# Experts' activations multiplied by their gates in halves of 128 tokens, the first half during the gates' stage; flags summed on VectorE; a deeper list pipeline

## The chip, the cores and the metric

The kernel runs on one core of a Trainium2 chip. What counts is the device time of one execution in microseconds; of several executions of one kernel the median is taken. Below, TensorE is PE in the profile, VectorE is DVE, ScalarE is ACT, GpSimd is POOL, and SP issues the weight loads.

## The reference, cut to what matters

256 tokens with 2048 features pass one attention block, then a layer of 16384 tiny experts, then a second block (a gated recurrence and projections). The change touches the middle layer alone:

```python
q = (xt @ w_query).reshape(T, 8, 2, 128)
scores = jnp.einsum('thpc,hpnc->thpn', q, sub_keys)
vals, idx = lax.top_k(scores, 16)
cand = (vals[..., 0, :, None] + vals[..., 1, None, :]).reshape(T, 8, 256)
top_vals, top_c = lax.top_k(cand, 16)
experts = (i1 * 128 + i2).reshape(T, 128)
gates = jax.nn.softmax(top_vals, axis=-1).reshape(T, 128)
hdn = gelu(einsum('ted,td->te', expert_down[experts], xc))
y = einsum('te,ted->td', gates * hdn, expert_up[experts])
```

## The kernel before, in words

The kernel does not gather the rows of `expert_down`. It multiplies the normalised tokens by all 16384 rows, takes the gelu, and multiplies by a gate matrix that is zero where a token did not choose an expert. Rows of `expert_up` are gathered, but only of experts that some token chose.

**Stream.** Every weight comes as a unit of 1 MB (`Stream`, L48). SP loads it into one of three `raw` tiles; ACT casts each half to a high part (L74) and DVE subtracts that part to get the low one (L75); five half tiles `whl` are in turn. `next()` makes the halves a unit needs, `used()` makes one more half after the unit's matmuls. `fm` (L91) then issues 48 matmuls of 256 columns (L100 to L102) for a unit.

**Order of the work.** Small steps beside the matmuls stand in a list `k.bg`. After each unit `pump` runs one step, and `pump_by(k, us)` (L172) runs steps against a credit: the unit gives `us`, each step takes the price it is declared with. `after(k, n, f)` puts f off by n pumps, `drain` runs all that is left. Every engine works its own instructions in the order in which they were written; nothing reorders them.

**The stages of the middle layer** (`phase_peer`, L563):
1. 16 query units. Scores go to the two-step top-16 on DVE (`topk`, L605). During the 16th unit the activations `act` are rewritten in place in four quarters (`split`, L209, from a copy `xr` scaled on POOL), each once the unit's matmuls of that quarter are done; the expert units read the new ones.
2. 128 expert units (`ORDER`, four units to a group j of 512 experts; JS=31 is the last group but one to be computed). Each unit's result passes the gelu on ACT (L982, in `hidden`).
3. Beside them, the gates' stage: 64 steps `place_steps` (L726), four tokens each: one-hot tiles on DVE (L690, L691), gates put in on ACT and DVE (L698, L700), four matmuls, copy on ACT (L717), addition on DVE (L722). After four steps the 16 tokens' tile `gst` (two in turn) goes to `used` (L736): POOL issues a store to `g_d` in HBM, and a DMA that adds the tile onto `fsum`; after eight tiles DVE reduces `fsum` to flags F (L744).
4. Beside the later expert units, the lists: 32 steps `lists_steps` (L848), each with one-hot tiles on DVE (L826, L828), ACT (L836) and DVE (L837) putting keys in, and four matmuls of 200 columns (L845). In step q the one-hots are those of q+2, the keys those of q+1, the matmuls those of q. What is left at unit 123 is drained.
5. A group of activations that is finished before all gates are placed is stored to `gh_d`; it is "late". Afterwards `catch_up` (L998) loads late groups and their gates again (`load_late`, `load_g`), multiplies them on POOL (`times`, L880) and stores them to `hm_d` (L883). Groups finished later are multiplied at once in `hidden`. JS is kept in SBUF as `hst` and split there, at once.
6. `overflow` (L1058) is a loop for more chosen experts than the lists hold, skipped if there are none; all engines read the count and branch. DVE computes two small tiles (L1060, L1062) ahead of the branch.
7. Four units of `expert_up` for JS and 100 gathered units (L1117).

Of the kernel before, what the change touches and what calls it, by code (L numbers as in the profile page):

```python
# [9 lines left out]
F32 = mybir.dt.float32  # L10
# [16 lines left out]
NE = 128  # L27
# [20 lines left out]
class Stream:  # L48
# [514 lines left out]
def phase_peer(k, A):  # L563
# [5 lines left out]
    with ExitStack() as ctx:  # L569
# [78 lines left out]
        slot, F = {}, []  # L648
# [30 lines left out]
        fsum = pp.tile([128, 128, 16], F32, name="fsum", tag="gtd")  # L679
# [141 lines left out]
        def lists_hot(q):  # L821
            cs = slice(4 * q, 4 * q + 4)
            a = pw.tile([128, 4, 128], F32R, name="oa", tag="oa", bufs=3)
# [8 lines left out]
        def lists_keys(q):  # L832
            cs = slice(4 * q, 4 * q + 4)
            b = pw.tile([128, 4, 2, KT], F32R, name="ob", tag="ob")
            e = hot[q][1]
            nc.scalar.mul(b[:, :, 0, :], e, pi)  # L836
            nc.vector.tensor_mul(b[:, :, 1, :], e, iota[:, cs, None].to_broadcast([128, 4, KT]))  # L837
            hot[q][1] = b

        def lists_fill(q):  # L840
# [3 lines left out]
            for j in range(4):  # L844
                nc.tensor.matmul(L["ps"][:, :2 * KT], a[:, j, :], b[:, j].rearrange("p e r -> p (e r)"),  # L845
                                 start=q + j == 0, stop=q == 31 and j == 3)

        def lists_steps(q):  # L848
# [4 lines left out]
            lists_fill(q)  # L853
# [17 lines left out]
        Gs, late = {}, deque()  # L871

        def load_g(m, tag):
            gt = pp.tile([128, 16, 128], F32, name="gt", tag=tag)
            nc.gpsimd.dma_start(gt, g_d[:, :, m * 128:(m + 1) * 128].rearrange("g p x -> p g x"))
# [6 lines left out]
        def store(j, gh):  # L882
            nc.gpsimd.dma_start(hm_d[1 + 512 * j:1 + 512 * (j + 1), :].rearrange("(a p) t -> p a t", p=128), gh)  # L883

        def load_late(j):
            if j // 2 not in Gs:
                Gs.clear()
                Gs[j // 2] = load_g(j // 2, "gst%d" % (j // 2 % 2))
            x = pp.tile([128, 4, 256], F32, name="ght", tag="ght%d" % (j % 3))
            nc.gpsimd.dma_start(x.rearrange("p a t -> p (a t)"), gh_d[j])  # L890
            return x, Gs[j // 2]
# [5 lines left out]
        scaled = []  # L897
        for g in range(16):
            w = st.next()
            acc = bank(k, "acc")[:, :256]  # L900
            if g == 15:
                for q in range(4):
                    fm(k, acc, w, k.act, part=(4 * q, 4 * q + 4))
                    qs = slice(4 * q, 4 * q + 4)
                    split(k, k.act[0][:, qs, :], k.act[1][:, qs, :], scaled.pop(0))
            elif g == 0:
# [16 lines left out]
            if g < 2:  # L923
                pump(k)
            else:
                pump_by(k, 3.2)
# [11 lines left out]
        state = {}  # L938

        def prepare():  # L940
# [30 lines left out]
            yield step(1.5, lambda: lists_hot(0))  # L971
            yield step(2.2, lambda: (lists_hot(1), lists_keys(0)))
            for q in range(32):
                yield step(2.2, lambda q=q: lists_steps(q))
# [5 lines left out]

        def hidden(j, a, gh, acc):
# [3 lines left out]
            if "placed" not in state:  # L985
                nc.scalar.dma_start(gh_d[j], gh.rearrange("p a t -> p (a t)"))
                late.append(j)
                return
            if state.get("g") != j // 2:
# [722 lines left out]
```

## Time and profile before

| | us |
|---|---|
| median of 3 runs | 2737.36 (lowest 2737.03) |
| the profiled execution | 2741.86 |
| its span, first to last instruction | 2740.1 |
| PE busy | 2634.3 (96%) |
| DVE busy | 1829.5 (67%) |
| ACT busy | 1411.4 (52%) |
| POOL busy | 738.6 (27%) |

The profiled execution is 4.5 us above the median, and 1.8 us of it lie outside the span. Busy shares are means over stages that differ; a stretch of the trace tells more. Where matmuls follow each other without a gap, their count in 50 us says how fast PE really went.

### The profile page before, as it was taken

What the parts mean: (1) busy time and instruction counts of PE and PEld (TensorE: products, weight loads), DVE (VectorE), ACT (ScalarE), POOL (GpSimd) and SP (SyncE); (2) the same over time, 40 slices, a digit from 0 to 9 for tenths busy, and PEclk for the clock granted to TensorE, in tenths of its full rate; (3) what the DMA queues carried; (4) which work ended last, traced back from release to release, by engine and by line L of the source; (5) the groups of instructions that cost most, each with busy time, mean ns of one, the idle gap of its engine ahead of it and who ended that gap; (6) DMA issues with size and microseconds to landing.
All of it is one profiled execution on the core that took longest, in us unless ns stands there. A gap on an engine that the chain in (4) does not pass through costs nothing. (4 is left out here: it accounts for less than half of the span.)

```text
span 2740.1 us, 44958 instructions
## 1 busy us (share of the span) xinstructions
PE 2634.3 (96%) x18008; PEld 2409.1 (88%) x18008; DVE 1829.5 (67%) x2685; ACT 1411.4 (52%) x2302; POOL 738.6 (27%) x779
## 2 busy tenths in 40 slices
PE   8999999989999999989759999999999999999997
PEld 8977778989999999989748888887999999999886
DVE  5554455899777877688826666666568775555555
ACT  6344455544566666434325555556665544444453
POOL 0001011532000000255625555645145540000000
PEclk9999999999999999999879999999999999999999
DMA  7433435456688888989847888885544445555553
GB/s 290 169 123 139 155 118 188 155 171 214 208 279 274 279 279 289 312 308 340 303 146 271 297 292 293 293 300 173 191 167 156 153 154 204 185 185 188 185 192 127
DMA packets 95268, 599.11 MB, mean 219 GB/s; under 512 B 11536, under 2 KB 11664, under 8 KB 31952
## 3 DMA queue, kind: packets, MB, share of 16 engines
q1 hardware_dynamic: 53696, 381.05, 39.6%
q0 software_dynamic: 36608, 200.23, 21.6%
q10 hardware_dynamic: 4752, 14.92, 1.5%
q8 instruction: 143, 2.34, 0.3%
q14 instruction: 69, 0.57, 0.1%
HBM read 532.19 MB, written 47.19 MB: 211 GB/s over the span
## 5 line engine op out<-in xcount | busy, mean ns | idle before, releaser
L75 DVE TENSOR_TENSOR whl<-raw,whl 128x1024 fp32r<-128x1024 f32 (+2 forms) x917 | 1188.5, 1306 | 633.7 <-ACT whl L74 623.0
L74 ACT CAST whl<-raw 128x1024 fp32r<-128x1024 f32 (+2 forms) x917 | 954.3, 1048 | 734.2 <-PE acc L102 381.4
L100 PE MATMUL acc<-act,whl 128*128 128x256 f32 x3840 | 1083.4, 282 | 17.8 <-ACT whl L74 17.6
L101 PE MATMUL acc<-act,whl 128*128 128x256 f32 x3840 | 1081.8, 282 | 9.1 <-DVE act L214 8.7
L102 PE MATMUL acc<-act,whl 128*128 128x256 f32 x3840 | 1081.6, 282 | 0.8 <-DVE whl L75 0.8
L100 PEld LDWEIGHTS acc<-act,whl 128*128 128x128 f32 x3840 | 729.4, 190 | 20.2 <-ACT whl L74 17.8
L101 PEld LDWEIGHTS acc<-act,whl 128*128 128x128 f32 x3840 | 730.1, 190 | 10.0 <-DVE act L214 8.9
L102 PEld LDWEIGHTS acc<-act,whl 128*128 128x128 f32 x3840 | 733.3, 191 | 1.3 <-DVE whl L75 1.3
L1117 PE MATMUL acc<-whl,hh 128*128 128x512 f32 x864 | 218.2, 396 | 0.0
L1117 PE MATMUL bg<-whl,hh 128*128 128x512 f32 x864 | 217.9, 396 | 0.0
L118 PE MATMUL acc<-whl,act 128*128 128x512 f32 (+1 forms) x512 | 198.2, 387 | 6.9 <-ACT whl L74 6.9
L119 PE MATMUL acc<-whl,act 128*128 128x512 f32 (+1 forms) x512 | 196.1, 383 | 4.0 <-DVE whl L75 3.9
L1117 PEld LDWEIGHTS bg<-whl,hh 128*128 128x128 f32 x864 | 162.5, 188 | 39.3
L1117 PEld LDWEIGHTS acc<-whl,hh 128*128 128x128 f32 x864 | 162.4, 188 | 39.2
L120 PE MATMUL acc<-whl,act 128*128 128x512 f32 (+1 forms) x512 | 195.8, 382 | 0.8 <-DVE act L217 0.8
L1047 POOL DMA_INDIRECT raw<-in_up,idx_l x100 | 134.1, 1341 | 150.5 <-DVE hh L895 77.6
L118 PEld LDWEIGHTS acc<-whl,act 128*128 128x128 f32 x512 | 97.5, 190 | 28.7 <-ACT whl L74 7.4
L119 PEld LDWEIGHTS acc<-whl,act 128*128 128x128 f32 x512 | 97.5, 190 | 24.4 <-DVE whl L75 5.8
L738 POOL DMA_DIRECT2D g_d<-gst x16 | 8.9, 556 | 395.7 <-DVE gst L722 395.7
L120 PEld LDWEIGHTS acc<-whl,act 128*128 128x128 f32 x512 | 97.4, 190 | 20.2 <-DVE act L217 1.0
L1047 POOL DMA_INDIRECT hr<-hm_d,idx_l x100 | 104.4, 1044 | 31.0 <-issue 30.7
L700 ACT ACTIVATE ob<-oe,sl_g 128x128 fp32r<-128x128 f32 x256 | 81.5, 391 | 8.1 <-ACT ghs L982 6.5
(407 smaller groups left out, 3071.5 us busy)
## 6 DMA issues: line engine op xcount, KB each, us to landing
raw<-in_down SPq DMA_DIRECT2D x128, 1024.0 KB, 6.3
raw<-in_w_cv SPq DMA_DIRECT2D x32, 1024.0 KB, 4.8
raw<-in_w_gg SPq DMA_DIRECT2D x32, 1024.0 KB, 4.8
raw<-in_w_dil SPq DMA_DIRECT2D x24, 1024.0 KB, 4.9
gt<-g_d POOLq DMA_DIRECT2D x17, 1024.0 KB, 10.7
raw<-in_w_out SPq DMA_DIRECT2D x16, 1024.0 KB, 4.8
raw<-in_w_pq SPq DMA_DIRECT2D x16, 1024.0 KB, 4.9
g_d<-gst POOLq DMA_DIRECT2D x16, 1024.0 KB, 7.8
```

The lines of the kernel that those rows point to most:

```text
L74: nc.scalar.copy(hi[:, s], r[:, s])
L75: nc.vector.tensor_sub(lo[:, s], r[:, s], hi[:, s].bitcast(F32))
L100: k.nc.tensor.matmul(acc, hi[:, f], x, start=j == 0, stop=False)
L101: k.nc.tensor.matmul(acc, hi[:, f], y, start=False, stop=False)
L102: k.nc.tensor.matmul(acc, lo[:, f], x, start=False, stop=j == nk - 1)
L118: k.nc.tensor.matmul(accs[t], ah[:, kk, ts], hi[:, m], start=st, stop=False)
L119: k.nc.tensor.matmul(accs[t], ah[:, kk, ts], lo[:, m], start=False, stop=False)
L120: k.nc.tensor.matmul(accs[t], al[:, kk, ts], hi[:, m], start=False, stop=sp)
L700: nc.scalar.mul(b[:, j, 0, :], e[:, j, :], slot["g"][:, 0, 4 * q + j:4 * q + j + 1].bitcast(F32))
L738: nc.gpsimd.dma_start(g_d[g], x.rearrange("p i t -> p (i t)"))
L1047: nc.gpsimd.indirect_dma_start(out=out, out_offset=None, in_=table, in_offset=bass.IndirectOffsetOnAxis(ap=idx, axis=0), bounds_check=n - ...
L1117: nc.tensor.matmul(accs[2 * s + c][t], x[:, ts], y[:, c * 512:(c + 1) * 512], start=i == 0 and x is hh and y is hi, stop=last_ and i == N - 1)
```

## The change

- `used`: no DMA onto `fsum`. DVE reduces each 16-token tile itself (128x2048 to 128x128) and adds the result to F. After tile 7 the first 128 tokens' gates count as placed (`placed0`), after tile 15 the others (`placed1`).
- The late groups are handled by halves of 128 tokens, with two lists. A first half may be loaded, multiplied and stored from `placed0` on, in two units of three, while the gates' stage still runs; second halves from `placed1` on, as before. Gate tiles are halves too; for a group multiplied at once, the next pair's gates are loaded as soon as the current pair is used.
- The lists: both key columns are put in by ACT (six instructions a step where there was one; DVE's L837 goes); the matmuls in step q are those of q-1; buffers are added under other tiles' tags; the declared price of a step falls from 2.2 to 1.7. Two of three waiting steps ahead of the lists go.
- JS's split into `hst` comes three pumps later.
- The last two query units run as a pair, quarter by quarter, so each quarter of `act` is rewritten while both go on; the two units get one step of background each.
- `overflow`: the two tiles are computed inside the branch.

```diff
         def used(g, x):
             nc.gpsimd.dma_start(g_d[g], x.rearrange("p i t -> p (i t)"))
-            if g % 8 == 0:
-                nc.gpsimd.dma_start(fsum, x)
-            else:
-                nc.gpsimd.dma_start(fsum, x, accum_op=OP.add)
+            f = F[g // 8] if g % 8 == 0 else pw.tile([128, 128], F32, name="fg", tag="tk")
+            nc.vector.tensor_reduce(f, x, axis=AX.X, op=OP.add)
+            if g % 8:
+                nc.vector.tensor_add(F[g // 8], F[g // 8], f)
             if g % 8 == 7:
-                after(k, 3, lambda: nc.vector.tensor_reduce(F[g // 8], fsum, axis=AX.X, op=OP.add))
+                state["placed%d" % (g // 8)] = True
...
         def lists_keys(q):
-            b = pw.tile([128, 4, 2, KT], F32R, name="ob", tag="ob")
+            if q % 3 == 2:
+                b = [pw.tile([128, 2, 2, KT], F32R, name="ob", tag="oh") for _ in range(2)]
+            else:
+                b = pw.tile([128, 4, 2, KT], F32R, name="ob", tag="ob")
+                b = [b[:, 0:2], b[:, 2:4]]
             e = hot[q][1]
-            nc.scalar.mul(b[:, :, 0, :], e, pi)
-            nc.vector.tensor_mul(b[:, :, 1, :], e, iota[:, cs, None].to_broadcast([128, 4, KT]))
+            for i in range(2):
+                nc.scalar.mul(b[i][:, :, 0, :], e[:, 2 * i:2 * i + 2], pi)
+            for j in range(4):
+                nc.scalar.mul(b[j // 2][:, j % 2, 1, :], e[:, j, :], float(4 * q + j))
...
-            lists_fill(q)
+            if q >= 1:
+                lists_fill(q - 1)
...
-        def load_late(j):
...
+        def load_late(j, t):
+            if j // 2 not in Gs[t]:
+                Gs[t].clear()
+                Gs[t][j // 2] = load_g(j // 2, t, "gst%d" % (j // 2 % 2) if t else "gtd", 1 if t else 2)
+            x = pp.tile([128, 4, 128], F32, name="ght", tag="ght%d" % (lates[0] % 3))
+            lates[0] += 1
+            nc.gpsimd.dma_start(x, gh_d[j].rearrange("p (a t) -> p a t", t=256)[:, :, t * 128:(t + 1) * 128])
+            return x, Gs[t][j // 2]
...
+                pair = [(acc, w), (bank(k, "acc")[:, :256], st.peek())]
                 for q in range(4):
-                    fm(k, acc, w, k.act, part=(4 * q, 4 * q + 4))
+                    for o, x in pair:
+                        fm(k, o, x, k.act, part=(4 * q, 4 * q + 4))
+                    if q == 1:
+                        st.used()
+                        st.used()
...
-            for q in range(32):
-                yield step(2.2, lambda q=q: lists_steps(q))
+            for q in range(33):
+                yield step(1.7, lambda q=q: lists_steps(q))
...
+            n = ORDER.index(j) + 1
+            if n < 32 and ORDER[n] // 2 != j // 2:
+                state["g"], state["gt"] = ORDER[n] // 2, [load_g(ORDER[n] // 2, t, "gtd", 2) for t in range(2)]
             if j == JS:
...
-                split(k, hst[:, 0], hst[:, 1], gh)
+                after(k, 3, lambda: split(k, hst[:, 0], hst[:, 1], gh))
...
+            n = 0
+            if "placed1" in state:
+                n = -(-(len(late[0]) + len(late[1])) // max(1, NE - 6 - i))
+            elif "placed0" in state and i % 3 < 2:
+                n = 1
...
-            nc.vector.tensor_scalar(d, d, -128.0 * KT, None, op0=OP.add)
...
-            with k.tc.If(turns > 0), k.tc.For_i(0, turns, 1) as _:
+            with k.tc.If(turns > 0):
+                nc.vector.tensor_scalar(d, d, -128.0 * KT, None, op0=OP.add)
```

**Where the order moves.** On VectorE, four steps of the gates' stage end with a finished 16-token tile. Before, `gst` is the tile, `oe`, `oa` and `ob` the one-hots and gates of the coming steps:

```order
L722 TENSOR_TENSOR gst<-gst,bg 128x128x2 x2
L690 TENSOR_TENSOR oe<-cst,sl_i_7110 128x512
L691 TENSOR_TENSOR oa<-cst,sl_i_7105 128x512
L698 TENSOR_TENSOR ob<-oe,sl_g 128x4x128
L75 TENSOR_TENSOR whl<-raw,whl 128x1024 x2
```

The changed kernel, at the end of a tile (`fg` is that tile's sum over its 16 tokens):

```order
L726 TENSOR_TENSOR gst<-gst,bg 128x128x2 x2
L744 TENSOR_REDUCE fg<-gst 128x128
L746 TENSOR_TENSOR F_7291<-F_7291,fg 128x128
L694 TENSOR_TENSOR oe<-cst,sl_i_7283 128x512
L695 TENSOR_TENSOR oa<-cst,sl_i_7278 128x512
L702 TENSOR_TENSOR ob<-oe,sl_g 128x4x128
L75 TENSOR_TENSOR whl<-raw,whl 128x1024 x2
```

A reduction and an addition stand ahead of the next step's one-hots, once in four units.

On GpSimd, the second half of the gates' stage, before:

```order
L738 DMA g_d<-gst 128x2048
L742 DMA fsum<-gst 128x2048
L738 DMA g_d<-gst 128x2048
L742 DMA fsum<-gst 128x2048
L738 DMA g_d<-gst 128x2048
```

The same place in the changed kernel (`ght` is a late group's half, `gt` its gates):

```order
L742 DMA g_d<-gst 128x2048
L893 TENSOR_TENSOR ght<-ght,gt 128x512
L896 DMA hm_d<-ght 128x4x128
L906 DMA ght<-gh_d 128x4x128
L893 TENSOR_TENSOR ght<-ght,gt 128x512
L896 DMA hm_d<-ght 128x4x128
L888 DMA gt<-g_d 128x8x128
L906 DMA ght<-gh_d 128x4x128
L893 TENSOR_TENSOR ght<-ght,gt 128x512
L896 DMA hm_d<-ght 128x4x128
L742 DMA g_d<-gst 128x2048
```

Between two stores of a gate tile there are now two or three multiplications with their loads and stores; 20 of them stand between the eighth and the sixteenth store.

On VectorE in the lists, before:

```order
L826 TENSOR_TENSOR oe<-cst,lrp 128x400
L828 TENSOR_TENSOR oa<-cst,lrp 128x512
L837 TENSOR_TENSOR ob<-oe,cst 128x4x100
L826 TENSOR_TENSOR oe<-cst,lrp 128x400
L828 TENSOR_TENSOR oa<-cst,lrp 128x512
L837 TENSOR_TENSOR ob<-oe,cst 128x4x100
L75 TENSOR_TENSOR whl<-raw,whl 128x1024 x2
```

The changed kernel's VectorE in the lists:

```order
L832 TENSOR_TENSOR oe<-cst,lrp 128x400
L834 TENSOR_TENSOR oa<-cst,lrp 128x512
L832 TENSOR_TENSOR oe<-cst,lrp 128x400
L834 TENSOR_TENSOR oa<-cst,lrp 128x512
L75 TENSOR_TENSOR whl<-raw,whl 128x1024 x2
```

A list step has two instructions on VectorE instead of three (and six on ScalarE instead of one). The keys are put in between the 102nd and the 120th gelu, where before that ran from the 101st to the 123rd.

## Rows read from the trace of the kernel before

**Rows 1.** Windows: stretch, its length, then PE, PEld, DVE, ACT, POOL, PEclk, DMA, GB/s

```profile
550.00:600.00 50.00, 41.27 (x330) 41.07 (x331) 48.26 (x113) 22.69 (x31) 19.41 (x15) 0.90 0.50 167
...
900.00:950.00 50.00, 50.00 (x429) 50.00 (x428) 40.52 (x57) 34.19 (x76) 2.91 (x4) 1.00 0.84 274
...
1200.00:1250.00 50.00, 39.47 (x293) 39.10 (x293) 39.00 (x32) 16.86 (x24) 30.81 (x24) 0.86 0.89 299
```

**Rows 2.** Waits, 500 to 700 us and 1100 to 1460: total us, times, longest

```profile
PE acc L101 <- DVE act L214: 8.7, 1, 8.7
...
POOL ght L880 <- DMA ght<-gh_d: 51.7, 11, 13.6
...
ACT hst L213 <- POOL ghs L880: 28.2, 1, 28.2
PE bg L845 <- DVE ob L837: 26.2, 9, 6.7
...
PE acc L100 <- ACT whl L74: 17.6, 1, 17.6
PE bg L1117 <- DVEq L1064: 13.3, 1, 13.3
```

**Rows 3.** Timeline of DVE and of POOL in the lists: start, us, instruction

```profile
1303.66 2.90 DVE L826 TENSOR_TENSOR oe<-cst,lrp 128x400 f32<-128x400 f32 x1
...
1307.08 0.56 DVE L837 TENSOR_TENSOR ob<-oe,cst 128x400 fp32r<-128x400 f32 x1
...
1303.77 2.35 POOL L880 TENSOR_TENSOR ght<-ght,gt 128x1024 f32<-128x1024 f32 x1
```

**Rows 4.** DVE by line and shape, 700 to 1100 us (gates' stage): busy us, mean ns

```profile
L75 DVE TENSOR_TENSOR whl<-raw,whl 128x1024 fp32r<-128x1024 f32 x133 | 162.2, 1222 | 79.8 <-ACT whl L74 79.8
...
L744 DVE TENSOR_REDUCE F<-fsum 128x128 f32<-128x2048 f32 x1 | 2.3, 2280 | 0.0
```

**Rows 5.** DVE by line and shape, 1180 to 1360 us (lists)

```profile
L75 DVE TENSOR_TENSOR whl<-raw,whl 128x1024 fp32r<-128x1024 f32 x45 | 79.1, 1779 | 22.3 <-ACT whl L74 22.2
L826 DVE TENSOR_TENSOR oe<-cst,lrp 128x400 f32<-128x400 f32 x32 | 36.8, 1151 | 1.1 <-ACT ob L836 0.4
L828 DVE TENSOR_TENSOR oa<-cst,lrp 128x512 fp32r<-128x512 f32 x32 | 26.2, 818 | 0.0
L837 DVE TENSOR_TENSOR ob<-oe,cst 128x400 fp32r<-128x400 f32 x30 | 23.7, 789 | 0.0
```

**Rows 6.** POOL: multiplications, 1140 to 1400 us; one 128x512 product of the top-16

```profile
L880 POOL TENSOR_TENSOR ght<-ght,gt 128x1024 f32<-128x1024 f32 x23 | 63.6, 2764 | 51.9 <-DMA ght<-gh_d 51.7
L880 POOL TENSOR_TENSOR ghs<-ghs,gt 128x1024 f32<-128x1024 f32 x8 | 20.0, 2499 | 62.5 <-DMA gt<-g_d 31.5 <-issue 18.5 <-ACT ghs L982 12.5
...
507.81 1.30 POOL L634 TENSOR_TENSOR oh<-oh,xf 128x512 f32<-128x512 f32 x1 [2.61 <-DVE oh L632]
```

**Rows 7.** ACT by line and shape: two of the lists, one of the gates' stage

```profile
L74 ACT CAST whl<-raw 128x1024 fp32r<-128x1024 f32 x44 | 45.9, 1046 | 73.7 <-PE acc L102 73.7
L836 ACT ACTIVATE ob<-oe,cst 128x400 fp32r<-128x400 f32 x31 | 19.2, 622 | 27.8 <-DVE oe L826 25.4 <-PE bg L845 2.3
...
L700 ACT ACTIVATE ob<-oe,sl_g 128x128 fp32r<-128x128 f32 x248 | 78.9, 391 | 7.7 <-ACT ghs L982 6.1 <-DVE oe L690 1.7
```

**Rows 8.** PE by line, 1180 to 1360 us: the lists' matmuls

```profile
L845 PE MATMUL bg<-ob,oa 128*128 128x200 f32 x120 | 20.5, 298 | 30.9 <-DVE ob L837 25.6 <-ACT ob L836 5.3
```

**Rows 9.** Timeline: gelus 101 and 128 on ACT; DVE around the branch

```profile
1178.67 0.38 ACT L982 ACTIVATE ghs<-acc 128x256 f32<-128x256 f32 x1
...
1408.31 0.38 ACT L982 ACTIVATE ghs<-acc 128x256 f32<-128x256 f32 x1 [2.07 <-PE acc L102]
...
1415.12 0.52 DVE L1062 TENSOR_SCALAR xe<-cst 128x128 f32<-128x128 f32 x1 [7.77 <-DMA hm_d<-ghs]
1421.57 1.22 DVE L75 TENSOR_TENSOR whl<-raw,whl 128x1024 fp32r<-128x1024 f32 x1 [5.94 <-DVEq L1064]
```

**Rows 10.** The chain that ended last, first matmuls behind the branch

```profile
1421.53 5.29 PE bg L1117 x12
```

More of the change, by code (lines that the diff above doesn't have):

```diff
@@ L984, in hidden @@
                 return
-            if "placed" not in state:
+            if "placed1" not in state:
                 nc.scalar.dma_start(gh_d[j], gh.rearrange("p a t -> p (a t)"))
-                late.append(j)
+                late[0].append(j)
+                late[1].append(j)
                 return
+            while late[0] or any(t == 0 for _, t, _ in pend):
+                if not pend:
+                    pend.append((late[0][0], 0, load_late(late[0].popleft(), 0)))
+                settle()
@@ L1007, in catch_up @@
+            if "placed1" in state:
+                n = -(-(len(late[0]) + len(late[1])) // max(1, NE - 6 - i))
+            elif "placed0" in state and i % 3 < 2:
+                n = 1
+            while pend and (len(pend) > 1 or not late[0] and not (late[1] and "placed1" in state)):
+                settle()
             for _ in range(min(n, 2 - len(pend))):
[L1008 to L1010 removed]
+                t = 0 if late[0] else 1
+                if late[t] and "placed%d" % t in state:
+                    j = late[t].popleft()
+                    pend.append((j, t, load_late(j, t)))
@@ L1028, in phase_peer @@
                 drain(k)
-        assert not k.bg and not late and not pend
+        assert not k.bg and not late[0] and not late[1] and not pend
         early.close()
@@ L1055, in phase_peer, with overflow_tile @@
         k.gather = gather
+        def overflow_tile(d, ex):
+            ps = bank(k, "bg")
+            for c in range(NE):
+                a = pw.tile([128, 128], F32, name="xa", tag="xa")
+                nc.vector.tensor_scalar(a, iota, d[:, c:c + 1], None, op0=OP.is_equal)
+                nc.tensor.matmul(ps[:, :1], a, ex[:, c:c + 1], start=c == 0, stop=c == NE - 1)
+            v = pp.tile([128, 1], F32, name="xv")
+            nc.vector.tensor_copy(v, ps[:, :1])
+            idx = indices(v, 1, "x")
+            x = pw.tile([128, 2048], F32, name="xu", tag="xu", bufs=1)
+            get(x, up, idx[:, 0, :], NE * 128)
+            y = pw.tile([128, 256], F32, name="xh", tag="hr", bufs=4)
+            get(y, hm_d, idx[:, 1, :], JS * 512 + 1)
+            h = pw.tile([128, 2, 256], F32R, name="xs", tag="hh", bufs=3)
+            split(k, h[:, 0], h[:, 1], y)
+            for c in range(4):
+                cs = slice(c * 512, (c + 1) * 512)
+                w = pw.tile([128, 2, 512], F32R, name="xw", tag="xw", bufs=1)
+                split(k, w[:, 0], w[:, 1], x[:, cs])
+                for t in range(2):
+                    ts = slice(t * 128, (t + 1) * 128)
+                    o = bank(k, "bg")
+                    for i, (p, q) in enumerate(((0, 0), (0, 1), (1, 0))):
+                        nc.tensor.matmul(o, h[:, p, ts], w[:, q], start=i == 0, stop=i == 2)
+                    nc.vector.tensor_add(k.h[:, t, cs], k.h[:, t, cs], o)
+            nc.vector.tensor_scalar(d, d, -128.0, None, op0=OP.add)
@@ L1090, in phase_peer @@
+            with k.tc.If(turns > 0):
+                nc.vector.tensor_scalar(d, d, -128.0 * KT, None, op0=OP.add)
+                ex = pw.tile([128, 128], F32, name="xe", tag="xe", bufs=1)
+                nc.vector.tensor_scalar(ex, iota, 128.0, pi, op0=OP.mult, op1=OP.add)
+                with k.tc.For_i(0, turns, 1) as _:
+                    overflow_tile(d, ex)
         overflow()
```

103 lines of the change are left out of this document (34 added, 69 removed).

## The prediction

> **What bounds the kernel now.** I read the page first: PE is busy for 96% of the span, so a gain can only come from the stretches where PE does not run at its full pace. The windows of 50 us show which these are [rows 1]. At full pace PE issues 429 matmuls in 50 us, 0.1166 us each; so a unit's 48 take 5.59 us. From 550 to 600 us only 330 are issued, which is 50 x (1 - 330/429) = 11.5 us lost; from 1200 to 1250 only 293, at a granted clock of 0.86. The second thing to read is what PE waited for there [rows 2]: 8.7 us for a VectorE split of `act` (the last query unit), 26.2 us for VectorE's keys in the lists, 17.6 us for a weight cast on ACT, and 13.3 us at the branch ahead of the overflow loop. ACT's cast is late because ACT stands 28.2 us in front of it, at JS's split, for POOL's multiplication.
>
> The loss in the lists is larger than these waits. Gelu 101 stands at 1178.67 us and gelu 128 at 1408.31 [rows 9]: 27 units in 229.6 us. At full pace they take 27 x 5.59 = 151.0 us, and the 128 matmuls of 200 columns between 128 x 0.1166 x 200/256 = 11.7 us and 128 x 20.5/120 = 21.9 us [rows 1, 8]. So 57 to 67 us are lost there. The third view says to whom. A VectorE instruction of 128x400 takes 0.56 us, but 2.90 when it starts while POOL multiplies for 2.35 us [rows 3]: it stands until POOL is done. Against undisturbed 1.222 us [rows 4] a weight subtraction takes 1.779 in the lists [rows 5]: 45 x 0.56 = 25 us; L826 loses 32 x 0.59 = 19 us, L837 30 x 0.23 = 7 us, L828 some 3 us (a 128x512 at 0.56 x 512/400 = 0.72). Together that is 54 us in 180. POOL's 31 multiplications in 260 us [rows 6] are 21.5 in 180 us, and 21.5 x 2.35 = 50 us: nearly the whole of POOL's time is taken from VectorE.
>
> Per unit (22.5 in 180 us, so 8.0 us each) VectorE's demand is 2 x 1.22 for the weights, 1.42 list steps x (0.56 + 0.72 + 0.56) = 2.62, and 0.95 x 2.35 = 2.24 under POOL: 7.3 us, where PE would want 6.1. The remaining tenth (8.0/7.3 = 1.10) are waits in a ring of ACT, PE and VectorE. VectorE, shared with POOL, bounds the lists.
>
> **The change part by part.**
>
> *Lists.* The order has 33 steps in 19 units (1.74 a unit). VectorE then asks for 2.44 + 1.74 x (0.56 + 0.72) = 4.67 us. POOL multiplies one second half a unit and two halves of a fresh group in four units, 1.5 halves; half of 2.35 is 1.18 and a 128x512 product took 1.30 [rows 6], so 1.27 is taken: 1.90. The sum is 6.57 us. PE asks for 5.59 + 1.74 x 4 x 0.091 = 6.23. ACT gets six key instructions for one: two of 200 columns at about 0.4 us (between L836's 0.622 for 400 and L700's 0.391 for 128) and four of 100 columns at no more than 78.9/248 = 0.32 us start to start [rows 7]; with two casts of 1.046 and a gelu of 0.38 [rows 9] that is 2.47 + 1.74 x 2.08 = 6.1 us. Three engines stand within 6%, so no gain beyond PE's 6.23 is to be had, and with the old tenth on top a unit would take 7.2. I take 6.6, since the keys now have two steps instead of one between ACT and PE. The last 8 units have no lists and take 5.59: JS's gates are loaded a group ahead and the split stands three pumps later, so the 28.2 us wait of ACT has 16 us of other units and a landed load in front of it, and the drain finds only the last copy. So 19 x 6.6 + 8 x 5.59 = 170.1 us instead of 229.6: **59.5 us gained** (66.5 at 6.23, 48 at 7.2).
>
> *Gates' stage.* A unit here has 52 matmuls, 6.06 us. VectorE is busy 40.52 of 50 us, 4.91 us a unit [rows 1]. A reduction of 2.28 us [rows 4] and an addition (about 0.3, less than the 0.56 of 128x400) once in four units add 0.65: 5.56 us, under 6.06, and hidden. What is hidden would show as a late subtraction: VectorE has waited 79.8 us in 400 for ACT, so it is there in time and one such 2.6 us is made good in two units. After `placed0` 20 half multiplications fall on 30 units: 0.67 x 1.27 = 0.85, together 6.41 us, 0.35 above PE's 6.06. Over 30 units that is 10.5 us, of which about a unit's lead is there beforehand. I take **6 us lost**. The ends are 0 and, with the lists' tenth, 30 x (6.41 x 1.10 - 6.06) = 30 us. The `fsum` DMAs that go were waited for by nobody on PE.
>
> The rows say that VectorE's additions and products of SBUF tiles stand still under POOL [rows 3]; for a reduction no row shows it. [...]
>
> *The query pair.* The first split of `act` moves ahead of two weight subtractions and one top-16 step (4 to 5 us of VectorE), but the 16th unit's weights, subtracted in the same queue, are now wanted a unit earlier, so PE waits for these instead. **5 us gained**; the ends are 0 and the whole 11.5.
>
> *The branch.* VectorE no longer stands 7.77 us for the last store ahead of `xe`, nor computes it (0.52). Its 5.94 us in the branch stay [rows 9], and PE goes on only when VectorE has passed. That takes 8.3 us from the gap of 13.3. The first 12 matmuls behind the gap took 5.29 us [rows 10], where 12 of 512 columns take 12 x 2 x 0.1166 = 2.8; of these 2.5 us a little may come back. **9 us gained**, between 5 (if PE's own jump, hidden in the gap, is longer) and 15.8 (if all goes).
>
> *Nothing, or covered:* the two waiting steps less (the pair pushes the steps back by as much: lists begin at gelu 102 instead of 101), the halves' extra DMA issues on POOL (POOL is 27% busy), smaller rows of DMA (the DMA engines are at 0.84 in the gates' stage, and `fsum`'s traffic goes).
>
> Sum: 59.5 + 5 + 9 - 6 = 67.5 us. The profiled execution took 2741.9 us (span 2740.1 and 1.8 around it); less 67.5 is 2674.4. The runs' median lies 4.5 us lower, so **2670 us**, 2.5% faster. Its own range, with 48 to 66 in the lists and 0 to 15 lost in the gates' stage, is 2655 to 2688.
>
> **The rivals.**
>
> *Port as before (A).* POOL multiplies as long as before (62 halves x 1.27 = 79 us, before 31 x 2.35 = 73), only earlier, where VectorE has little left. If the ring's tenth stays in the lists (7.2 a unit: 48 us) and appears in the gates' stage (15 us lost), with 2 for the pair and 7 for the branch, the gain is 42 and the time 2695. For it: the three demands within 6%. Against: one more step of depth, and steps in two per unit.
>
> *POOL's queue holds back the gate tiles (B), the slower side.* POOL works in order, and the store of a finished gate tile now stands behind two or three multiplications, each of which waits for its load. The steps cannot start on a tile whose store before last has not landed. A group of four units lasts 24.2 us, with 2.67 halves: from 9.1 us a half POOL sets the pace. The longest wait for such a load was 13.6 us [rows 2]; with 1.27 for the product 2.67 x 14.9 = 39.7 us a group, 15.5 more, x 8 = 124 us. In place of the 6 us lost that makes 2670 - 6 + 124 = 2788, 1.9% slower than before; it is slower than before at all from 12.5 us a half. Against: a load is issued two turns ahead, about 12 us, so most of the wait is past.
>
> *Everything hidden (C).* Lists at PE's pace (66.5), the gates' stage free, the pair's whole 11.5, 12 at the branch: 90 us, 2647.
>
> **How the numbers follow.** Forecast 0.58, A 0.24, C 0.12, B 0.06. A change of 2% (54.7 us, to 2682.6) is about what a measurement of this kernel can tell from no change. Seven eighths of the forecast's range lie below that: faster 0.51 + 0.12 = 0.63; same 0.07 + 0.24 + 0.03 = 0.34; slower, half of B, 0.03. The range of 8 in 10 reaches from C to A and a little beyond: 2647 to 2702.
>
> **What would show it.** Right: some 6.6 us between gelus 102 and 120, and 5.6 after; no 28 us wait of ACT at JS's split; PE's gap at the branch near 5 us; VectorE over 47 of 50 us in the second half of the gates' stage, PE there still above 410 matmuls in 50 us. Wrong: gelus over 7.5 us apart in the lists (A); waits of `gst` copies for stores, or gaps of many us between gate tiles (B); a VectorE with slack in the gates' second half, so that POOL's time was not taken from it. ACT's key instructions above 0.4 us each would move the bound of the lists to ACT.

## The result, and the profile after

| | before | after |
|---|---|---|
| median, us | 2737.66 (4 runs) | 2668.80 (2665.95 to 2671.98, 4 runs) |
| ratio | | 0.9744 (95%: 0.9729 to 0.9759) |
| profiled execution / span, us | 2741.86 / 2740.1 | 2668.61 / 2666.8 |
| PE busy | 2634.3 (96%) | 2621.0 (98%) |
| DVE busy | 1829.5 (67%) | 1850.6 (69%) |
| POOL busy | 738.6 (27%) | 797.9 (30%) |

The changed kernel is 2.6% faster; 2670 us was predicted. One of the four executions of before took 6640 us; it counts in this median, but not in the ratio, which compares fast executions alone. Line numbers shift: the expert units' matmuls are now L105 to L107, the lists' L856, the gelu L1009, the multiplication by gates L893.

First the windows of the changed kernel, in the columns of [rows 1]: window and its length, busy time of PE, PEld, DVE, ACT and POOL with the instructions counted, granted clock, DMA share, GB/s.

```profile
550.00:600.00 50.00, 45.47 (x362) 44.88 (x361) 44.80 (x93) 24.40 (x34) 16.30 (x12) 0.93 0.51 175
...
950.00:1000.00 50.00, 49.85 (x425) 49.67 (x424) 47.51 (x61) 32.99 (x72) 23.43 (x23) 1.00 0.96 335
1000.00:1050.00 50.00, 48.73 (x416) 48.55 (x416) 48.15 (x58) 32.99 (x72) 21.45 (x23) 1.00 0.90 319
1050.00:1100.00 50.00, 50.00 (x429) 50.00 (x428) 47.58 (x61) 33.35 (x73) 22.09 (x21) 1.00 0.86 304
1100.00:1150.00 50.00, 48.74 (x417) 48.57 (x416) 42.26 (x54) 27.52 (x52) 21.52 (x22) 1.00 0.94 330
...
1200.00:1250.00 50.00, 48.59 (x416) 48.45 (x415) 48.20 (x40) 35.06 (x99) 39.55 (x36) 1.00 0.93 322
```

TensorE's full pace is 429 matmuls in 50 us [rows 1]. In the lists (1200 to 1250) it now issues 416 at full clock, where it issued 293 at 0.86. The query window went from 330 to 362: 32 x 0.1166 = 3.7 us back. The second half of the gates' stage is where something is lost: 4 + 13 + 0 + 12 matmuls are missing from 950 to 1150, 3.4 us, with VectorE busy for 47.5 to 48.2 of 50 us in three of the four windows.

The waits of the changed kernel, 500 to 700 us (first row) and 1100 to 1460 us; columns as in [rows 2].

```profile
PE acc L107 <- DVE whl L75: 3.5, 2, 3.3
...
POOL ght L893 <- DMA ght<-gh_d: 30.8, 11, 5.5
...
PE bg L1160 <- PEq L1126: 2.6, 1, 2.6
...
PE bg L856 <- DVE oa L834: 1.4, 1, 1.4
```

The wait for the split of `act` became one of 3.3 us for the pair's second unit of weights. The 26.2 us for keys, the 17.6 for a cast and the 28.2 of ScalarE at JS [rows 2] have no successor; TensorE stands 2.6 us at the branch, where it stood 13.3. Loads of late halves are waited for 5.5 us at the longest, where it was 13.6.

The timeline shows the same on four ScalarE instructions and one of TensorE (start, us, engine, line): gelus 101 and 121, JS's split, gelu 128, first matmuls behind the branch.

```profile
1179.98 0.38 ACT L1009 ACTIVATE ghs<-acc 128x256 f32<-128x256 f32 x1
...
1311.03 0.37 ACT L1009 ACTIVATE ghs<-acc 128x256 f32<-128x256 f32 x1
...
1338.63 1.04 ACT L218 CAST hst<-ghs 128x1024 fp32r<-128x1024 f32 x1
...
1345.84 0.38 ACT L1009 ACTIVATE ghs<-acc 128x256 f32<-128x256 f32 x1 [1.44 <-PE acc L107]
...
1348.36 3.04 PE L1160 MATMUL bg<-whl,hst 128*128 128x512 f32 x12 [2.56 <-PEq L1126]
```

From gelu 101 to 128 it is 165.9 us, before 229.6 [rows 9]; gelu 102 stands at 1185.63, so the 19 units of the lists, from there to gelu 121, take 125.4 us, 6.60 each. JS's cast stands without a wait.

VectorE and GpSimd by line and shape in those lists, 1186 to 1311 us; columns as in [rows 5] and [rows 6].

```profile
L75 DVE TENSOR_TENSOR whl<-raw,whl 128x1024 fp32r<-128x1024 f32 x38 | 64.7, 1741 | 7.1 <-ACT whl L74 7.0
L834 DVE TENSOR_TENSOR oa<-cst,lrp 128x512 fp32r<-128x512 f32 x31 | 32.5, 1048 | 0.0
L832 DVE TENSOR_TENSOR oe<-cst,lrp 128x400 f32<-128x400 f32 x31 | 28.6, 924 | 0.0
...
L893 POOL TENSOR_TENSOR ght<-ght,gt 128x512 f32<-128x512 f32 x20 | 32.0, 1602 | 18.6 <-DMA ght<-gh_d 18.3
L893 POOL TENSOR_TENSOR ghs<-ghs,gt 128x512 f32<-128x512 f32 x10 | 17.3, 1752 | 0.1
```

The three VectorE groups add up to 125.8 us in 125 us (in the timeline an instruction's record begins 0.07 to 0.08 us before the one ahead of it ends; VectorE is busy for 119.5 us of the 125), with 7 us idle. So VectorE still sets the pace of the lists, and it is still stretched by GpSimd: a subtraction of 1.22 us takes 1.74.

### The profile page after: what moved, and what is told of

Read it like the earlier page. It is cut to its first block, busy times and chain, and to the rows that moved or that the text cites. A ratio compares the mean times of both kernels' runs of the same rounds, so it can differ in the third digit from the quotient of the medians.

```text
span 2666.8 us, 45194 instructions
## 1 busy us (share of the span) xinstructions
PE 2621.0 (98%) x18008; PEld 2395.4 (90%) x18008; DVE 1850.6 (69%) x2679; ACT 1438.8 (54%) x2462; POOL 797.9 (30%) x858
## 5 line engine op out<-in xcount | busy, mean ns | idle before, releaser
L107 PE MATMUL acc<-act,whl 128*128 128x256 f32 x3840 | 1076.7, 280 | 3.5 <-DVE whl L75 3.5
L105 PE MATMUL acc<-act,whl 128*128 128x256 f32 x3840 | 1077.8, 281 | 0.2
L107 PEld LDWEIGHTS acc<-act,whl 128*128 128x128 f32 x3840 | 728.3, 190 | 3.9 <-DVE whl L75 3.9
L105 PEld LDWEIGHTS acc<-act,whl 128*128 128x128 f32 x3840 | 722.9, 188 | 2.3 <-issue 1.2
L123 PEld LDWEIGHTS acc<-whl,act 128*128 128x128 f32 x512 | 97.7, 191 | 29.4 <-ACT whl L74 7.4
L893 POOL TENSOR_TENSOR ght<-ght,gt 128x512 f32<-128x512 f32 x46 | 76.9, 1673 | 44.2 <-DMA ght<-gh_d 43.7
```

The lines of the kernel that those rows point to most:

```text
L105: k.nc.tensor.matmul(acc, hi[:, f], x, start=j == 0, stop=False)
L107: k.nc.tensor.matmul(acc, lo[:, f], x, start=False, stop=j == nk - 1)
L123: k.nc.tensor.matmul(accs[t], ah[:, kk, ts], hi[:, m], start=st, stop=False)
L893: nc.gpsimd.tensor_mul(x, x, gt[:, (j % 2) * 4:(j % 2) * 4 + 4])
```

## The experiments

The kernel before, timed again beside these runs, took 2739.0 to 2741.2 us (medians).

**Is VectorE's time really taken by GpSimd's multiplications?** The kernel before, its multiplications by gates gone:

```diff
-            x = gh.rearrange("p a (g t) -> p a g t", t=16)
-            nc.gpsimd.tensor_mul(x, x, gt[:, (j % 2) * 4:(j % 2) * 4 + 4])
+            pass
```

> The kernel before with GpSimd's gate multiplications left out (31 of them; loads and stores stay). Port theory: VectorE's demand in the lists falls from 7.3 to 5.1 us a unit, PE (6.1) bounds, so gelu 101 to 128 takes about 170 us instead of 229.6, and the 28 us wait at JS's split is gone; about 2678 us (2665 to 2690). Rival, the shallow chain of keys (ACT to PE to VectorE in one step) makes the loss: units stay above 7.5 us, about 2720 us.

Measured: 2689.6 us, ratio 0.9816 (0.9800 to 0.9832). VectorE by line in its lists, 1180 to 1360 us:

```profile
L75 DVE TENSOR_TENSOR whl<-raw,whl 128x1024 fp32r<-128x1024 f32 x52 | 63.2, 1224 | 60.4 <-ACT whl L74 60.0
L828 DVE TENSOR_TENSOR oa<-cst,lrp 128x512 fp32r<-128x512 f32 x32 | 21.9, 685 | 0.0
L826 DVE TENSOR_TENSOR oe<-cst,lrp 128x400 f32<-128x400 f32 x32 | 18.3, 571 | 0.8
L837 DVE TENSOR_TENSOR ob<-oe,cst 128x400 fp32r<-128x400 f32 x32 | 18.1, 570 | 0.0
```

Every instruction is back at its undisturbed time: 1224 ns for 1779, 571 for 1151, 570 for 789 [rows 5]. The stretching was GpSimd's. 12 us less than expected came back; what holds them is not shown. The windows show where to look, for the DMA engines are now full:

```profile
1200.00:1250.00 50.00, 48.19 (x411) 47.90 (x410) 33.69 (x45) 23.02 (x33) 12.09 (x16) 1.00 1.02 383
...
1350.00:1400.00 50.00, 34.91 (x154) 28.44 (x154) 19.54 (x20) 17.98 (x23) 13.21 (x14) 0.83 0.54 180
```

VectorE has slack (33.7 of 50 us), but loads and stores follow each other at a DMA share of 1.02, and TensorE still stands 15.1 us at the branch.

**The parts alone.** The new lists (with price 1.7) in the kernel before, and the old ones in the kernel after; the core of the edit:

```diff
-            nc.vector.tensor_mul(b[:, :, 1, :], e, iota[:, cs, None].to_broadcast([128, 4, KT]))
+            for j in range(4):
+                nc.scalar.mul(b[j // 2][:, j % 2, 1, :], e[:, j, :], float(4 * q + j))
...
-            lists_fill(q)
+            if q >= 1:
+                lists_fill(q - 1)
...
-            for q in range(32):
-                yield step(2.2, lambda q=q: lists_steps(q))
+            for q in range(33):
+                yield step(1.7, lambda q=q: lists_steps(q))
```

> The kernel before with the new lists alone (keys on ACT, matmuls one step later, price 1.7). Port theory: demand 2.44 + 2.22 + 2.4 under POOL = 7.1 us a unit, and the drain is nearly empty, JS's wait of 17.6 us stays: gelu 101 to 128 about 203 us, 2711 us in all (2700 to 2722). Rival, the chain of keys: nearly the whole gain of the lists, about 2685 us.

> The changed kernel with the old lists (keys on ACT and VectorE, three instructions a step on VectorE, price 2.2). Port theory: demand 2.44 + 2.62 + 1.9 = 7.0 us a unit, with a tenth on top 7.6, some units more in the lists and some us in the drain: 25 to 35 us more than the changed kernel, about 2698 us (2688 to 2712). Rival, the chain of keys: it loses the whole gain of the lists, about 2725 us.

Measured: the new lists alone 2742.6 us, ratio 1.0007 (0.9996 to 1.0018), so nothing, and both expectations fell. The old lists in the changed kernel 2705.3 us, 0.9880 (0.9863 to 0.9898), 36.5 us above the changed kernel, within the range of what the expectations call the port theory: VectorE, standing still while GpSimd multiplies, bounds the lists. The runs show the standing still, not what causes it; "port" is only a name for it. One part is worth nothing alone and 36 us beside the others. The waits of the first of these runs, 1160 to 1460 us, say where the time stayed:

```profile
ACT ghs L990 <- DMA hm_d<-ghs: 52.5, 4, 17.5
POOL ghs L888 <- DMA gt<-g_d: 47.8, 4, 17.3
ACT hst L213 <- POOL ghs L888: 44.8, 1, 44.8
...
PE acc L100 <- ACT whl L74: 36.4, 2, 34.2
```

GpSimd works a chain in order: gate loads, loads of late groups, multiplications and stores, with 31 multiplications in all. ScalarE's gelu writes into `ghs`, of which there are three, and waits for the store of an older one (52.5 us); at JS it waits for the multiplication itself (44.8), and TensorE for ScalarE's cast behind that. JS's multiplication starts at 1398.78 us; in the kernel before at 1393.95. So I formed a second theory: GpSimd's chain is a second bound, hidden right behind VectorE's.

**The branch alone.** The kernel before with the two small tiles computed inside the branch:

```diff
-            nc.vector.tensor_scalar(d, d, -128.0 * KT, None, op0=OP.add)
-            ex = pw.tile([128, 128], F32, name="xe", tag="xe", bufs=1)
-            nc.vector.tensor_scalar(ex, iota, 128.0, pi, op0=OP.mult, op1=OP.add)
...
-            with k.tc.If(turns > 0), k.tc.For_i(0, turns, 1) as _:
...
+            with k.tc.If(turns > 0):
+                nc.vector.tensor_scalar(d, d, -128.0 * KT, None, op0=OP.add)
+                ex = pw.tile([128, 128], F32, name="xe", tag="xe", bufs=1)
+                nc.vector.tensor_scalar(ex, iota, 128.0, pi, op0=OP.mult, op1=OP.add)
...
```

> The kernel before with the two small tiles computed inside the branch. Both theories: PE's gap at the branch falls from 13.3 us to about 2.6 and the clock stays up, 11 to 13 us less: 2726 us (2723 to 2730). If the gap was PE's own jump: no change, 2737.

Measured: 2726.8 us, 0.9951 (0.9935 to 0.9968): 12.8 us, as expected. The first matmuls behind the branch, in the chain that ended last:

```profile
1410.12 3.04 PE bg L1122 x12
```

They take 3.04 us instead of 5.29 [rows 10], as in the changed kernel. The windows over these matmuls say why; they are those of the kernel before, of the changed kernel and of the changed kernel with price 2.0 (a run told of further down):

```profile
1421.50:1426.50 5.00, 4.97 (x12) 3.94 (x13) 1.22 (x1) 0.00 (x0) 0.00 (x0) 0.50 0.00 2
...
1348.00:1352.00 4.00, 3.64 (x16) 2.99 (x17) 1.79 (x1) 0.62 (x2) 1.61 (x3) 1.00 0.40 135
...
1344.80:1350.00 5.20, 5.17 (x12) 4.14 (x13) 1.05 (x1) 0.00 (x0) 2.52 (x3) 0.50 0.40 120
```

TensorE's granted clock is 0.50 in the kernel before, and 1.00 in the changed one. But the edit does not secure that: in nine runs that have it TensorE stood 2.4 to 3.0 us at the branch, and five of them (price 2.0, old lists, old pair, products on VectorE, a half in every unit) still took 4.39 to 5.46 us for these 12 matmuls, at a granted clock of 0.50 to 0.66 in the mean. What decides it is open.

**Testing GpSimd's chain.** The kernel before with the two edits at JS alone, and the same with the new lists:

```diff
+            n = ORDER.index(j) + 1
+            if n < 32 and ORDER[n] // 2 != j // 2:
+                state["g"], state["gt"] = ORDER[n] // 2, load_g(ORDER[n] // 2, "gtd")
             if j == JS:
...
-                split(k, hst[:, 0], hst[:, 1], gh)
+                after(k, 3, lambda: split(k, hst[:, 0], hst[:, 1], gh))
```

> The kernel before with two edits alone: JS's split three pumps later, and a fresh group's gates loaded as soon as the pair ahead of it is used. Theory 1 (the wait at JS is a price of its own): ScalarE no longer stands 28 us, TensorE's 17.6 us wait for its cast goes, and nothing else moves: 2722 us. Rival (GpSimd's chain of gate loads and multiplications ends JS, and what ScalarE does not lose there it loses in the lists, where VectorE is blocked the more as GpSimd waits less for gates): under 5 us gained, 2735 or more.

> The kernel before with the new lists and price 1.7 and with the two edits at JS, still whole groups and all multiplied after the gates' stage. Theory 1 (GpSimd's in-order chain, with 48 us of waits for gates in the run of the lists alone, was the second bound behind which the lists' gain vanished): those waits go, ScalarE's 45 us wait at JS goes, and the lists bring about 36 us on top of the other edits: 2690 us (2680 to 2700). Rival (the chain is bound by its late groups' loads and multiplications themselves, and only halves handled in the gates' stage free the lists): not more than 10 us better than the two JS edits alone, 2715 or more.

Measured: 2726.2 us, 0.9934 (0.9910 to 0.9958), for the JS edits; 2714.0, 0.9898 (0.9877 to 0.9919), with the lists. The wait at JS is a price of its own, 13 us of the 17.6 expected; but three runs of the JS edits lie at 2726 to 2729 us and two at 2717, so that its size is known to some 10 us only. On top of its median the lists bring 12 us, not the 36 that they bring beside halves: nearer to the rival, with the chain bound by its late groups. GpSimd's multiplication for JS in the JS-edits run, in the timeline:

```profile
1373.00 3.16 POOL L880 TENSOR_TENSOR ghs<-ghs,gt 128x1024 f32<-128x1024 f32 x1 [13.79 <-ACT ghs L982]
```

With the old lists GpSimd waits 13.8 us for ScalarE: its chain is ahead. In the run with the new lists, GpSimd and then ScalarE:

```profile
1359.70 2.38 POOL L888 TENSOR_TENSOR ght<-ght,gt 128x1024 f32<-128x1024 f32 x1 [9.85 <-DMA ght<-gh_d]
...
1377.52 2.33 POOL L888 TENSOR_TENSOR ghs<-ghs,gt 128x1024 f32<-128x1024 f32 x1 [6.29 <-DMA gt<-g_d]
...
1369.28 0.38 ACT L990 ACTIVATE ghs<-acc 128x256 f32<-128x256 f32 x1 [20.54 <-DMA hm_d<-ghs]
```

Here GpSimd waits for its loads, reaches JS 4.5 us later than there, and a gelu stands 20.5 us for a store of that chain, with the casts for TensorE behind it. Gelus 102 and 120 of this run, and TensorE's wait at the branch, show where the lists' gain went:

```profile
1187.75 0.37 ACT L990 ACTIVATE ghs<-acc 128x256 f32<-128x256 f32 x1
...
1310.07 0.37 ACT L990 ACTIVATE ghs<-acc 128x256 f32<-128x256 f32 x1
...
PE bg L1128 <- DVEq L1075: 30.8, 1, 30.8
```

The lists themselves are as fast as in the changed kernel (122.3 us between these gelus, there 121.8), so a faster VectorE in the lists is not what the halves bring. TensorE is done with the expert units 29.5 us earlier than with the JS edits alone, at 1361.6 us, and then stands 30.8 us at the branch instead of 13.5, while ScalarE and VectorE ahead of it wait for GpSimd's stores and for JS: 17 of the 29.5 us are lost there. In the changed kernel, where 20 half multiplications of the chain lie in the gates' stage, JS's multiplication starts at 1327.67 us and waits 7.7 us for ScalarE: the chain is ahead again. So this is what the halves are for, and why the parts don't add: with the branch, pair and JS edits in place (their 13, 4 and 13 us taken off, an estimate from these runs and the one below that takes the parts to add up and is known to some 10 us), whole groups with old lists would take 2710 us and with new lists 2698; halves with old lists took 2705, with new lists 2669. By this estimate the halves (with the flags) alone bring 5 us, the lists alone 12, both 41. Whether the order of GpSimd's queue or the DMA engines behind it hold the chain back is not shown: with whole groups and new lists the DMA share is 0.94 to 1.00 from 1200 to 1350 us, in the changed kernel 0.93, 0.92 and 0.75.

**The pair.** The changed kernel with the query stage of before:

```diff
...
-            if g == 14:
-
-                pair = [(acc, w), (bank(k, "acc")[:, :256], st.peek())]
...
+            if g == 15:
                 for q in range(4):
-                    for o, x in pair:
-                        fm(k, o, x, k.act, part=(4 * q, 4 * q + 4))
...
+                    fm(k, acc, w, k.act, part=(4 * q, 4 * q + 4))
...
```

> The changed kernel with the query stage of before: the 16th query unit alone walks through its quarters, no pair. Theory 1 (the windows of 550 to 600 us): 3.7 us come back, 2672.5 us. Rival (the two units also shift the gates' stage by a unit and take steps away): under 2 us of difference either way, 2667 to 2671.

Measured: 2672.4 us (2669.3 to 2675.2), 0.9748 (0.9728 to 0.9769), 3.6 us above the changed kernel. The intervals overlap, so the time alone doesn't settle it; its window 550 to 600 us is that of before:

```profile
550.00:600.00 50.00, 41.15 (x331) 40.75 (x330) 48.38 (x116) 22.97 (x32) 20.21 (x16) 0.90 0.47 155
```

331 matmuls against 362 is 3.6 us.

**What is lost in the gates' stage.** The changed kernel, late groups' first halves not multiplied:

```diff
-            times(x, gt, j)
+            if t:
+                times(x, gt, j)
```

> The changed kernel, but first halves of late groups are loaded and stored without being multiplied by their gates (the product of these 128 tokens with their gates is left out for late groups). Theory 1 (VectorE, stopped by GpSimd, bounds the second half of the gates' stage by a little): the 3.4 us lost from 950 to 1150 us come back, and VectorE's busy time there falls by 4 of 50 us: 2665 us, and at the lists nothing changes. Rival (what is lost there is the transfers' share of 0.9 or GpSimd's in-order queue): TensorE's matmuls per window stay at 416 to 429, and the time within 1 us of 2669.

Measured: 2666.9 us (2665.0 to 2670.8), 0.9732 (0.9711 to 0.9752): by the time alone unclear. The windows are clear:

```profile
950.00:1000.00 50.00, 50.00 (x428) 50.00 (x427) 43.40 (x60) 33.86 (x73) 12.79 (x17) 1.00 0.95 339
1000.00:1050.00 50.00, 50.00 (x429) 50.00 (x428) 44.65 (x61) 33.77 (x76) 12.07 (x16) 1.00 0.92 328
1050.00:1100.00 50.00, 50.00 (x429) 50.00 (x428) 44.82 (x64) 34.18 (x78) 12.03 (x16) 1.00 0.90 316
```

TensorE is at full pace at the same DMA share, so it was the multiplications, not transfers. Gelu 101 comes at 1175.53 us, 4.5 earlier. Of that 1.1 us stand ahead of the first gelu (581.25 against 582.32 us), where the two kernels do not differ yet. The other 3.4 us are what the changed kernel's windows miss. But from gelu 101 to 128 it takes 168.8 us, 2.9 more than in the changed kernel, which no row explains.

**Taking the halves faster.** The changed kernel with a first half in every unit:

```diff
-            elif "placed0" in state and i % 3 < 2:
+            elif "placed0" in state:
```

> The changed kernel with one first half a unit taken up in the gates' stage once the first 128 tokens are placed, and not in two units of three. Theory (each half takes 1.27 us of VectorE wherever it stands, and VectorE has 5.6 of TensorE's 6.06 us a unit filled there): some 5 to 8 more halves there overfill VectorE by 0.8 us a unit, about 10 us more are lost from 950 to 1150 us, and 5 to 8 halves fewer give back at most 8 in the lists: 2668 to 2676 us. Rival (only GpSimd's chain behind the gates' stage counts, and the shorter the faster): 5 us or more faster, 2664 or less.

Measured: 2668.1 us (2665.8 to 2669.0), 0.9732 (0.9715 to 0.9748), the changed kernel's time. Its premise failed: until 1160 us 24 late halves are multiplied instead of 23, since GpSimd soon waits for groups that are not finished yet (49.8 us, four times). They only come earlier:

```profile
950.00:1000.00 50.00, 48.47 (x407) 47.78 (x406) 49.90 (x56) 32.07 (x71) 28.75 (x31) 1.00 0.99 347
1000.00:1050.00 50.00, 47.07 (x398) 46.55 (x397) 49.86 (x58) 32.41 (x72) 27.46 (x30) 1.00 0.98 343
1050.00:1100.00 50.00, 48.94 (x418) 48.76 (x417) 48.99 (x64) 33.07 (x74) 15.68 (x17) 1.00 0.90 310
```

With VectorE at 49.9 of 50 us, 22 + 31 + 11 matmuls are lost, 7.5 us in place of 2 in these three windows.

**The multiplications on VectorE itself.**

```diff
-            nc.gpsimd.tensor_mul(x, x, gt[:, (j % 2) * 4:(j % 2) * 4 + 4])
+            nc.vector.tensor_mul(x, x, gt[:, (j % 2) * 4:(j % 2) * 4 + 4])
```

> The changed kernel with the multiplications by gates written on VectorE instead of GpSimd. Theory (a product costs VectorE its GpSimd time, some 1.27 us a half, and would cost it only about 0.7 by itself): VectorE asks for 0.6 x 1.5 = 0.9 us a unit less in the lists, 5.7 against TensorE's 6.2, so about 7 us come back there, and the 3.4 us of the gates' stage: 2658 us. Rival (VectorE now stands in its own queue for each half's load, where GpSimd waited 28.5 us beside it, and the weights behind it come late): some 20 us slower than the changed kernel, 2690.

Measured: 2675.7 us (2669.1 to 2676.7), 0.9755 (0.9739 to 0.9772): not faster than the changed kernel, and far from the rival's 2690. VectorE by line in its lists, 1186 to 1311 us:

```profile
L75 DVE TENSOR_TENSOR whl<-raw,whl 128x1024 fp32r<-128x1024 f32 x37 | 43.6, 1220 | 2.4 <-ACT whl L74 2.4
...
L893 DVE TENSOR_TENSOR ght<-ght,gt 128x512 f32<-128x512 f32 x19 | 13.1, 689 | 29.4 <-DMA ght<-gh_d 26.5 <-issue 2.9
```

Both theories saw half of it: a half costs 0.69 us and nothing is stretched any more, but VectorE stands 29.4 us in front of its products, 26.5 of them for loads.

**The price of a list step.** 2.0 and 1.85 instead of 1.7:

```diff
-                yield step(1.7, lambda q=q: lists_steps(q))
+                yield step(2.0, lambda q=q: lists_steps(q))
```

> The changed kernel with the declared price of a list step 2.0 instead of 1.7, so 1.5 steps a unit and not 1.74. Theory (VectorE shared with GpSimd bounds the lists, at 6.6 us a unit): VectorE's demand falls to 2.44 + 1.5 x 1.28 + 1.9 = 6.3 us a unit, level with TensorE's 6.1, over 22 units instead of 19; the sum of VectorE's work is the same, so 101 to 128 takes 163 to 167 us instead of 165.9: 2666 to 2669 us, no change that can be measured. Rival (the rest of the loss in the lists is waits for one-hots and keys, which fewer steps a unit relieve): 5 us or more faster, 2664 or less.

> The changed kernel with the price of a list step 1.85, between 1.7 (2668.8 us) and 2.0 (2663.9 us), where a step or two are left over for the drain. Theory (VectorE's shared time bounds the lists, and what price 2.0 gained is that its demand came under TensorE's, 6.3 to 6.1 us a unit): at 1.6 steps a unit the demand is 2.44 + 1.6 x 1.28 + 1.9 = 6.4 us against 6.2, so about half of the gain: 2666 us (2664 to 2668). Rival (what 2.0 gained is chance of the chips and runs): 2668 to 2671.

Measured: 2663.9 us (2661.5 to 2666.4), 0.9716 (0.9700 to 0.9732), at 2.0; 2662.0 (2661.4 to 2664.9), 0.9712 (0.9698 to 0.9726), at 1.85. The latter's interval lies just below the changed kernel's: it is the fastest kernel of this study, 0.3% ahead. Windows at 2.0:

```profile
1200.00:1250.00 50.00, 50.00 (x431) 50.00 (x430) 46.42 (x41) 36.12 (x97) 30.95 (x31) 1.00 0.92 314
1250.00:1300.00 50.00, 50.00 (x431) 50.00 (x431) 47.74 (x41) 35.06 (x97) 37.12 (x36) 1.00 0.97 333
```

The lists now run at TensorE's full pace. From gelu 101 to 128 it is 162.4 us at 2.0 and 164.7 at 1.85, 3.5 and 1.2 less than at 1.7. For 2.0 that is just below the theory's 163 to 167, while the time meets the rival's bound of 2664; at 1.85 both expectations lay too high, the theory's less. So VectorE's demand accounts for the lists, not for the whole gain. Of the rest, 0.5 and 3.0 us stand ahead of gelu 101, where the price has no part yet. At 1.85, 2.6 of the 3.0 are there at the first gelu already (579.77 against 582.32 us), up to which the programs are the same: from 460 to 480 us the granted clock was 1.00 in that run and 0.91 in the changed kernel. Seven runs have the pair and this same program, and their first gelus stand between 579.7 and 582.7 us. So differences of 2 or 3 us between two profiled executions say little by themselves, and how much of the 5 to 7 us by the medians is the price's stays open.

## Why the prediction came out right

**The bound of the lists: shown.** The reading that VectorE, shared with GpSimd, sets the lists' pace was tested from both sides: without multiplications every VectorE instruction is back at its time, and with the old lists in the changed kernel 36.5 us return. 6.6 us a unit was predicted and 6.60 measured. Of 59.5 us forecast, 63.8 came. The 4 us too few are a slip in the prediction's sum: the last 8 units were counted at 5.59 each, but gelu 128 follows 127 by 1.8 us, since no further unit stands between them, and the 229.6 us of before had that too. One of the three demands was mis-sized: the six key instructions were put at 2.08 us a step, and ScalarE comes to 5.1 us a unit rather than 6.1. It was never near being the bound. And one row was read too closely: the VectorE record of 2.90 us in [rows 3] begins 0.11 us ahead of GpSimd's and not inside it; that VectorE stands until GpSimd is done is shown by its end (1306.56 us, 0.44 behind GpSimd's 1306.12) and by the run without multiplications (the same instruction takes 0.571 us there).

**The branch: mis-sized.** 9 us forecast, 13.0 came: 10.7 from the gap (13.26 to 2.56) and 2.25 from the first 12 matmuls, where the clock stayed up, as it did in four of nine runs with this edit. The step that failed is that VectorE's 5.94 us in the branch stay and TensorE goes on only when VectorE has passed. In the changed kernel TensorE stands 2.56 us, for its own sequencer; VectorE's next instruction waits 2.71 us for ScalarE, no longer for the branch. The run of the branch alone measured 12.8 us.

**The query pair:** 5 us forecast, 3.7 by the windows, 2.6 by the first gelu (584.94 us before, 582.32 after); the new wait for the 16th unit's weights stands where the prediction put it (3.3 us).

**The gates' stage:** 6 us lost were forecast. From the first gelu to gelu 101 the changed kernel takes 3.9 us longer than the kernel before, 3.4 of them by the multiplications, as the run without them shows; the other 0.5 lie between the first two gelus. The cover of the reduction and the addition held: without the multiplications TensorE loses nothing (428 and 429 matmuls in the windows). Rival B did not come: the longest wait for a late load is 5.5 us.

**The sum.** 63.8 + 2.6 + 13.0 - 3.9 = 75.5 us, where 67.5 were forecast. At the second group of matmuls behind the branch the changed kernel is accordingly 75.4 us ahead (1426.66 against 1351.23 us); at the end it is 73.3. 1.6 of these 2 us are given back in one place some 480 us behind the branch, in the second block, which the change does not touch: the granted clock is 0.91 from 1820 to 1840 us in the changed kernel, and 1.00 in the same place before (1890 to 1910). By the medians, 2668.8 against 2737.66, 68.9 us remain, since the profiled execution of before lay some 4 us above its median. That the predicted 2670 is closer than its terms are is luck: the terms fall short by 8 us, of which 2.2 are given back and 4.4 are the slow profiled execution of before. Against the later medians of the kernel before (2739.0 to 2741.2) the gain is 70 to 72 us.

**What the prediction did not see** is the second bound. It treated the halves as a cost (the gates' stage) and the lists as a gain, each by itself. The runs show that the lists' gain reaches the end only because the halves shorten GpSimd's chain: new lists alone gave nothing, and with the JS edits 17 of 29.5 us were lost again at the branch. The prediction was spared since both came together; for a change with the lists alone the same working would have promised some 28 us, as my expectation for that run did, and been wrong.

## What to carry to other kernels

When a shared engine is relieved, ask which in-order chain ends next: here GpSimd's loads and multiplications stood right behind VectorE and swallowed the whole gain until part of them had moved to an earlier stage. Price a GpSimd product by what runs beside it on VectorE, not by its own duration alone: one of 1.3 us cost VectorE 0.8 us in the gates' stage here and 1.4 in the lists. And measure the parts of a change alone and left out: a part that is worth nothing alone can be worth 36 us beside the others, as the lists were here.

## What the runs showed of the hardware

**A reduction and a multiplication run side by side.** VectorE and GpSimd in the changed kernel's gates' stage, from the timeline:

```profile
1034.46 2.29 DVE L744 TENSOR_REDUCE fg<-gst 128x128 f32<-128x2048 f32 x1
...
1035.30 1.31 POOL L893 TENSOR_TENSOR ght<-ght,gt 128x512 f32<-128x512 f32 x1
...
1068.60 4.30 POOL L893 TENSOR_TENSOR ght<-ght,gt 128x512 f32<-128x512 f32 x1 [3.10 <-DMA ght<-gh_d]
...
1069.38 2.35 DVE L75 TENSOR_TENSOR whl<-raw,whl 128x1024 fp32r<-128x1024 f32 x2
1071.65 0.74 DVE L726 TENSOR_TENSOR gst<-gst,bg 128x256 f32<-128x256 f32 x2
```

The multiplication lies wholly inside the reduction, and both take their undisturbed time: 1.31 us against 1.30 [rows 6], and 2.29 against 2.28 [rows 4]. A multiplication of 1.30 to 1.32 us begins inside each of the eight reductions of 2.29 us from 960 to 1137 us; in five of them it also ends inside. This is the question that the prediction left open: where the two lay over each other here, neither took longer.

**The stretching goes both ways.** The product at 1068.60 takes 4.30 us instead of 1.30: VectorE's one-hots, products and subtractions run back to back until 1071.7 at their undisturbed time (0.68 us each, 2.35 for two subtractions), and GpSimd's product ends 1.25 us after VectorE has turned to additions that read a PSUM tile (`bg`). Those take 0.74 us for two, as elsewhere. From 950 to 1100 us the groups that are stretched work on SBUF tiles alone: in the mean 1.342 us a subtraction for 1.222 in the kernel before (700 to 1100 us), 0.892 a product (L702) for 0.683, 0.770 and 0.718 a one-hot for 0.683 and 0.684, 0.470 an addition onto F for 0.293 with the products on VectorE. The additions from PSUM take 0.411 for 0.415, the reductions 2.286 for 2.280. In the same stretch VectorE is busy 143.2 us with and 132.9 without the multiplications, for 178 instructions against 184. Group by group its 178 instructions are stretched by 14 us (6 of them on 48 subtractions), so the 17 multiplications there cost it 0.8 us each; in the lists, where VectorE has little else, the stretching is 38 x 0.52 + 31 x 0.36 + 31 x 0.35 = 42 us for 30, 1.4 us each. The prediction took 1.27 in both places.
